# Sixteen products of a group's eight SSD heads in one block instead of two blocks of eight

## The chip, the cores and the metric

One core of a Trainium2 chip runs the kernel in one launch. The metric is the device time of that launch in microseconds. Beside it stands a profile: one execution taken by the hardware profiler. The engines are TensorE (PE, with its weight loads as PEld), VectorE (DVE), ScalarE (ACT), GpSimd (POOL) and SyncE (SP, which issues the DMAs of the weights).

## What is computed

The kernel computes a decoder layer for 256 tokens of width 1024, all in float32: a SwiGLU, then two branches side by side (a Mamba-2 SSD and differential attention) that are merged through gates, then a second SwiGLU, with norms around each. The change lies in the SSD. It has 32 heads of 64 channels in 4 groups of 8 heads, a state of 128, and two chunks of 128 tokens. The part of the reference that matters, cut to it:

```python
X = (x.astype(jnp.float32) * dt[..., None]).reshape(b, nc, Q, G, E, P)
...
Lmat = jnp.exp(jnp.where(causal, seg, -jnp.inf))
CB = jnp.einsum('bclgn,bcsgn->bgcls', Cc, Bc)
y_diag = jnp.einsum('bgcls,bgecls,bcsgep->bclgep', CB, Lmat, X)
...
return (y_diag + y_off).reshape(b, L, H, P)
...
y = (y + d_skip.astype(jnp.float32)[:, None] * xh.astype(jnp.float32)).astype(z.dtype)
```

With only two chunks the kernel does not carry a state from one to the other. It treats a head as causal attention over 256 tokens without a softmax: a head's matrix E (decay times CB, three 128 x 128 blocks, since the fourth is zero) is multiplied with the head's X, and the skip term is added.

## The kernel before

The weights come in chunks of 1 MB. Each chunk is split into a high part (`whi`, a cast on ACT, line 168) and a low part (`wlo`, a subtraction on DVE, line 171), so that float32 products are made of three faster ones. The projections run one chunk after another on PE: the convolved inputs `pxs`, then `pz` for the gate z in eight chunks (`pz00` to `pz31`, 48 matmuls each, lines 204 to 207), then `pq` and `pk` by turns, then the gates, and so on.

The SSD is background work beside these projections. `ssd_work` is a generator that is advanced between the chunks by a planner with a time budget: each `yield` tells how many microseconds of work the step is taken to be. For each of the 4 groups it does the following.

- It transposes the group's x on PE into `px` and multiplies with dt on DVE into `X` (lines 881, 882).
- For each half of the group, four heads, it loads a row of cumulated decays, broadcast over all partitions, into `acb` (a DMA issued by POOL, line 890).
- For each pair of heads it makes `E`: six small operations on ACT and DVE, one exponential over both heads on ACT (line 261), and one multiplication with the masked CB on DVE (line 904). The pool of E has 4 buffers (`K3_BUFS`).
- At the end of each half it multiplies: 8 products into one PSUM tile `py` (line 913; each product shows as two records in the profile), and adds the skip term on DVE with two operations per half (line 921).

While this stage is built, PE's order is left to the scheduler of the framework, which places each instruction by its own estimates. ACT's and DVE's orders come from it as well. The products of one half are tied together by order dependencies with the reason "together", so that the scheduler cannot put projection matmuls between them. The tile `py` comes from the PSUM pool `bg`, which has 5 buffers of one bank each; the same pool holds `px` and the scores of the attention. After the groups come `ssd_norm`, which multiplies with silu(z) and normalizes, and the attention.

Of the kernel before, what the change touches and what calls it, by code (L numbers as in the profile page):

```python
# [17 lines left out]
ALU = mybir.AluOpType  # L18
# [6 lines left out]
P = 128  # L25
T = 256
# [22 lines left out]
def tile_hybrid_layer(ctx: ExitStack, tc: tile.TileContext, x, ffn1_pre_g, ffn1_w_gate, ffn1_w_up,  # L49
# [4 lines left out]
    nc = tc.nc  # L54
# [5 lines left out]
    def k4(shape, name, dt=F32):  # L60
        return sb.tile(shape, dt, tag="k4", name=name, bufs=K4_BUFS)

    def k3(shape, name, dt=F32):
        return sb.tile(shape, dt, tag="k3", name=name, bufs=K3_BUFS)
# [18 lines left out]
    def bg(shape, name):  # L83
        return ps.tile(shape, F32, tag="bg", name=name, bufs=5)
# [166 lines left out]
    order = mybir.DependencyInfo(mybir.DependencyClass.NoSync, mybir.DependencyReason.DATA)  # L251
# [8 lines left out]
    def act(*args, **kw):  # L260
        a = nc.scalar.activation(*args, **kw)
        if act_fence[0] is not None:
            tc.add_manual_dep(a.ins, act_fence[0], order, reason="activation table")
        act_since.append(a.ins.name)
# [453 lines left out]
    cols_b = const.tile([P, 112], F32, name="cols_b")  # L718
# [51 lines left out]
    for jj in range(2):  # L770
        for a in (uh, ul):
            for i in range(4):
                k = i * 2 + jj
                nc.tensor.matmul(pdt[i * H_SSD:(i + 1) * H_SSD, :], wdt[:, k, :], a(k).bitcast(F32),
                                 start=jj == 0 and a is uh, stop=jj == 1 and a is ul)
# [94 lines left out]
    xs = [None] * 4  # L870
# [4 lines left out]
    def ssd_work(groups):  # L875
        for g in groups:
            X = k4([P, 2, 512], f"X{g}")
            for b in range(2):
                px = bg([P, 4, P], f"px{g}{b}")
                for c in range(4):  # L880
                    nc.tensor.transpose(px[:, c, :], xs[g][:, c, b * P:(b + 1) * P], ident)
                nc.vector.tensor_tensor(
                    X[:, b, :].rearrange("p (e q) -> p e q", q=64),
                    px.rearrange("p c (e q) -> p (c e) q", q=64),
                    dt[:, b, g * 8:(g + 1) * 8].unsqueeze(2).to_broadcast([P, 8, 64]), ALU.mult)
                yield 0.6
            for hf in range(2):
                acb = k4([P, 4, T], f"acb{g}{hf}")
                r0 = g * 8 + hf * 4
                nc.gpsimd.dma_start(acb, acd[r0:r0 + 4, :].partition_broadcast(P))  # L890
                py = bg([P, 2, T], f"py{g}{hf}")
                Es = []
                for pr in range(2):
                    E = k3([P, 2, 3 * P], f"E{g}{hf}{pr}")
                    for i in range(2):
                        hd = r0 + pr * 2 + i
                        lh = pr * 2 + i
                        act(E[:, i, :P], acb[:, lh, P:], AF.Relu, bias=acs[:, 1, hd:hd + 1])
                        nc.vector.tensor_scalar(E[:, i, P:T], acb[:, lh, :P], acs[:, 0, hd:hd + 1], 0.0,
                                                ALU.add, ALU.max)  # L900
                        act(E[:, i, T:], acb[:, lh, P:], AF.Exp, bias=acs[:, 2, hd:hd + 1], scale=-1.0)
                    act(E[:, :, :T], E[:, :, :T], AF.Exp, scale=-1.0)
                    Es.append(E)
                    nc.vector.tensor_tensor(E, E, cbm[g].unsqueeze(1).to_broadcast([P, 2, 3 * P]), ALU.mult)
                    yield 1.4

                last = None
                for pr in (1, 0):
                    for keys in range(2):
                        for i in range(2):  # L910
                            xc = slice((hf * 4 + pr * 2 + i) * 64, (hf * 4 + pr * 2 + i + 1) * 64)
                            o = py[i * 64:(i + 1) * 64, pr, keys * P:]
                            m = nc.tensor.matmul(o, X[:, keys, xc], Es[pr][:, i, (1 - keys) * P:(3 - 2 * keys) * P],
                                                 start=keys == 0, stop=keys == 1)
                            if last is not None:
                                tc.add_manual_dep(m.ins, last.ins.name, order, reason="together")
                            last = m
                for pr in range(2):
                    c = hf * 2 + pr
                    dc = 96 + g * 4 + c  # L920
                    nc.vector.scalar_tensor_tensor(xs[g][:, c, :], xs[g][:, c, :], cols_b[:, dc:dc + 1],
                                                   py[:, pr, :], ALU.mult, ALU.add)
                yield 0.8

    def ssd_norm(groups):

# [211 lines left out]
    for g in range(4):  # L1138
        xs[g] = k4([P, 4, T], f"xs{g}")
        for i in range(2):  # L1140
# [3 lines left out]
            back.run(0.4)  # L1144
    act_table(EXP_LN)
    back.add(ssd_work(range(4)))
    for g in range(4):
        sz[g] = k4([P, 4, T], f"sz{g}")
# [10 lines left out]
    for c in range(4):  # L1159
# [3 lines left out]
        o = (c % 2) * 2  # L1163
# [138 lines left out]
```

## Time and profile before

| | us |
|---|---|
| time, median of 3 runs | 745.24 (745.14 to 746.96) |
| the profiled execution | 745.16 |
| its span | 743.4 |
| PE busy | 734.7 |
| DVE busy | 524.9 |
| ACT busy | 441.3 |
| products of line 913, PE busy | 12.2 |

The profiled execution's own time is 1.76 us longer than its span; the sum of a forecast is made against that execution. In a row of the timeline the first number is the start in the span, the second the time from the first start to the last end of what is merged in the row; then come engine, line, operation, the tiles written and read, the shape and the count. Matmuls overlap in the pipeline: one may be shown as 0.28 us long while the next starts 0.12 us after it, so starts tell more than lengths. What stands in brackets at the end is the engine's idle time and what ended it. PE's weight loads have rows of their own.

### The profile page before, as it was taken

Reading aid. Unit: us, or ns where it says so; the run is one execution under the profiler, and the core shown is the slowest. Engines: PE = TensorE matmul, PEld = TensorE weight load, DVE = VectorE, ACT = ScalarE, POOL = GpSimd, SP = SyncE. Lnnn points to the kernel's source line nnn. Section 1 sums busy time; section 2 is a strip of 40 time slices with the busy share of each in tenths; the row PEclk is TensorE's granted clock in tenths of the full one; section 3 lists DMA queues with packets and bytes.
Section 4 is the critical chain, followed back from the end, with each engine's and each line's share of the span. In section 5 each row is a group of like instructions: output and inputs, shape, how many; then the busy total and the mean of one; then the engine's idle time right before and its main releaser. Section 6 shows DMA issues by size and latency. Waiting matters only on the chain.

```text
span 743.4 us, 11055 instructions
## 1 busy us (share of the span) xinstructions
PE 734.7 (99%) x4369; PEld 641.3 (86%) x4369; DVE 524.9 (71%) x807; ACT 441.3 (59%) x742; POOL 37.8 (5%) x72
## 2 busy tenths in 40 slices
PE   8999999999999999999999999999999999999996
PEld 6888888888889999999999888888888888888885
DVE  7986567654577888767888998684774867766612
ACT  6665557543566565957967666782664655665512
POOL 2700000000200000000000000000010000000000
PEclk9999999999999999999999999999999999999998
DMA  8884676486253647574656555364470767644701
GB/s 297 225 265 152 206 227 254 174 281 226 64 170 116 202 140 233 168 221 148 197 174 218 173 175 210 127 236 189 135 241 22 226 227 227 190 172 183 277 1 56
DMA packets 94212, 137.96 MB, mean 186 GB/s; under 512 B 2684, under 2 KB 68304, under 8 KB 94160
## 3 DMA queue, kind: packets, MB, share of 16 engines
q1 hardware_dynamic: 91488, 129.51, 52.9%
q0 software_dynamic: 2368, 7.22, 3.2%
q8 instruction: 34, 0.56, 0.3%
q10 hardware_dynamic: 304, 0.53, 0.2%
q14 instruction: 18, 0.15, 0.1%
HBM read 136.17 MB, written 1.08 MB: 185 GB/s over the span
## 4 chain that ended last, share of the span: by engine, by line
PE 98%; DMA 0%; DVE 0%; issue 0%; ACT 0%; DVEq 0%
PE acc_f L470 16%; PE pup_f L219 9%; PE pg_f L219 9%; PE pws L234 6%; PE pgt L234 6%; PE pg_f L218 4%; PE pup_f L218 4%; PE pn_f L244 3%; PE pn_f L234 3%; PE acc_mx L470 3%; PE pn_mx L234 3%; PE pwd L234 3%; PE pz L207 2%; PE pxs L207 2%; PE pz L205 2%; PE pz L204 2%
## 5 line engine op out<-in xcount | busy, mean ns | idle before, releaser
L171 DVE TENSOR_TENSOR wlo<-raw,whi 128x1024 fp32r<-128x1024 f32 (+1 forms) x246 | 290.9, 1211 | 55.7 <-ACT whi L168 54.6
L168 ACT CAST whi<-raw 128x1024 fp32r<-128x1024 f32 (+1 forms) x245 | 247.2, 1047 | 55.3 <-PE acc_f L470 21.7
L219 PE MATMUL pg_f<-u_f,whi 128*128 128x512 f32 x288 | 101.3, 396 | 0.0
L219 PE MATMUL pup_f<-u_f,whi 128*128 128x512 f32 x288 | 101.1, 396 | 0.0
L218 PE MATMUL pg_f<-u_f,wlo 128*128 128x256 f32 x252 | 70.6, 280 | 0.0
L218 PE MATMUL pup_f<-u_f,wlo 128*128 128x256 f32 x252 | 70.3, 279 | 0.0
L219 PEld LDWEIGHTS pg_f<-u_f,whi 128*128 128x128 f32 x288 | 52.8, 188 | 9.7
L219 PEld LDWEIGHTS pup_f<-u_f,whi 128*128 128x128 f32 x288 | 52.7, 188 | 9.8
L470 PE MATMUL acc_f<-whi,gh_f 128*128 128x512 f32 x176 | 58.1, 390 | 0.0
L470 PE MATMUL acc_f<-whi,gl_f 128*128 128x512 f32 x176 | 58.1, 389 | 0.0
L470 PE MATMUL acc_f<-wlo,gh_f 128*128 128x512 f32 x176 | 58.1, 389 | 0.0
L218 PEld LDWEIGHTS pg_f<-u_f,wlo 128*128 128x128 f32 x252 | 47.5, 189 | 1.7
L218 PEld LDWEIGHTS pup_f<-u_f,wlo 128*128 128x128 f32 x252 | 47.5, 189 | 1.6
L223 DVE TENSOR_TENSOR su_f<-pup_f,su_f 128x256 f32<-128x256 f32 x36 | 15.2, 421 | 40.5 <-ACT su_f L222 40.5
L470 PEld LDWEIGHTS acc_f<-wlo,gh_f 128*128 128x128 f32 x176 | 33.0, 188 | 6.9
L470 PEld LDWEIGHTS acc_f<-whi,gl_f 128*128 128x128 f32 x176 | 33.0, 188 | 6.8
L470 PEld LDWEIGHTS acc_f<-whi,gh_f 128*128 128x128 f32 x176 | 33.0, 188 | 6.7
L234 PE MATMUL pgt<-whi,u_mx 128*128 128x512 f32 x128 | 33.1, 393 | 0.0
L222 ACT COPY su_f<-pup_f 128x256 f32<-128x256 f32 x36 | 13.4, 371 | 31.4 <-PE pup_f L219 31.2
L204 PE MATMUL pxs<-u_mx,whi 128*128 128x256 f32 x128 | 31.7, 285 | 0.0
L204 PE MATMUL pz<-u_mx,whi 128*128 128x256 f32 x128 | 31.6, 284 | 0.0
L205 PE MATMUL pz<-u_mx,whi 128*128 128x256 f32 x128 | 31.4, 283 | 0.0
(310 smaller groups left out, 1433.6 us busy)
## 6 DMA issues: line engine op xcount, KB each, us to landing
raw<-in_w_in_dram SPq DMA_DIRECT2D x40, 1024.0 KB, 5.4
raw<-in_ffn_w_down_dram SPq DMA_DIRECT2D x22, 1024.0 KB, 5.1
raw<-in_ffn_w_gate_dram SPq DMA_DIRECT2D x20, 1024.0 KB, 6.0
raw<-in_ffn_w_up_dram SPq DMA_DIRECT2D x20, 1024.0 KB, 5.4
raw<-in_ssd_w_branch_dram SPq DMA_DIRECT2D x8, 1024.0 KB, 5.1
acb<-acd POOLq DMA_DIRECT2D x8, 512.0 KB, 4.9
raw<-in_da_w_branch_dram SPq DMA_DIRECT2D x4, 1024.0 KB, 5.1
raw<-in_w_out_dram SPq DMA_DIRECT2D x4, 1024.0 KB, 4.9
```

The lines of the kernel that those rows point to most:

```text
L168: copy(hi[:, js, :], r[:, q * nj + j:q * nj + j + n, :])
L171: nc.vector.tensor_sub(lo[:, js, :], r[:, q * nj + j:q * nj + j + n, :], hi[:, js, :].bitcast(F32))
L204: nc.tensor.matmul(acc[m], wh(j)[:, cs], ah(k0 + j), start=first and j == ks[0], stop=False)
L205: nc.tensor.matmul(acc[m], wh(j)[:, cs], al(k0 + j), start=False, stop=False)
L207: nc.tensor.matmul(acc[m], wl(j)[:, cs], ah(k0 + j), start=False, stop=last and j == ks[-1])
L218: nc.tensor.matmul(acc[:, :T], wl(j)[:, cs], ah(j), start=False, stop=False)
L219: nc.tensor.matmul(acc, wh(j)[:, cs], ahl(j), start=j == 0, stop=j == KD - 1)
L222: nc.scalar.copy(dst[:, m, :], acc[:, T:])
L223: nc.vector.tensor_tensor(dst[:, m, :], acc[:, :T], dst[:, m, :], ALU.add)
L234: nc.tensor.matmul(acc, a(k0 + j), b(j), start=first and i == 0, stop=last and i == 11)
L244: nc.tensor.matmul(accs[b], x_(k0 + j), w_(j), start=first and j == 0 and w_ is wh and x_ is acts[b][0], stop=last and j == 3 and w_ is wl)
L470: nc.tensor.matmul(acc[b][q], x_[:, ts], w_(kt)[:, halves[q]], start=i == 0 and kt == 0 and x_ is ah and w_ is wh, stop=i == n - 1 and kt ...
```

## The change

The list of E is now kept for the whole group, so all four E (eight heads) are made first. Then two `py` tiles are taken and the group's 16 products are issued in one chain of order dependencies, from the last pair of heads to the first. The four additions of the skip term follow in the same order. The number of products, their operands and sizes are the same; the planner's two steps of 0.8 become one of 1.6.

```diff
+            Es = []
             for hf in range(2):
                 acb = k4([P, 4, T], f"acb{g}{hf}")
                 r0 = g * 8 + hf * 4
                 nc.gpsimd.dma_start(acb, acd[r0:r0 + 4, :].partition_broadcast(P))
-                py = bg([P, 2, T], f"py{g}{hf}")
-                Es = []
                 for pr in range(2):
...
-                last = None
-                for pr in (1, 0):
-                    for keys in range(2):
-                        for i in range(2):
-                            xc = slice((hf * 4 + pr * 2 + i) * 64, (hf * 4 + pr * 2 + i + 1) * 64)
-                            o = py[i * 64:(i + 1) * 64, pr, keys * P:]
-                            m = nc.tensor.matmul(o, X[:, keys, xc], Es[pr][:, i, (1 - keys) * P:(3 - 2 * keys) * P],
-                                                 start=keys == 0, stop=keys == 1)
-                            if last is not None:
-                                tc.add_manual_dep(m.ins, last.ins.name, order, reason="together")
-                            last = m
-                for pr in range(2):
-                    c = hf * 2 + pr
-                    dc = 96 + g * 4 + c
-                    nc.vector.scalar_tensor_tensor(xs[g][:, c, :], xs[g][:, c, :], cols_b[:, dc:dc + 1],
-                                                   py[:, pr, :], ALU.mult, ALU.add)
-                yield 0.8
+            py = [bg([P, 2, T], f"py{g}{hf}") for hf in range(2)]
+            last = None
+            for c in (3, 2, 1, 0):
+                for keys in range(2):
+                    for i in range(2):
+                        xc = slice((c * 2 + i) * 64, (c * 2 + i + 1) * 64)
+                        o = py[c // 2][i * 64:(i + 1) * 64, c % 2, keys * P:]
+                        m = nc.tensor.matmul(o, X[:, keys, xc], Es[c][:, i, (1 - keys) * P:(3 - 2 * keys) * P],
+                                             start=keys == 0, stop=keys == 1)
+                        if last is not None:
+                            tc.add_manual_dep(m.ins, last.ins.name, order, reason="together")
+                        last = m
+            for c in (3, 2, 1, 0):
+                dc = 96 + g * 4 + c
+                nc.vector.scalar_tensor_tensor(xs[g][:, c, :], xs[g][:, c, :], cols_b[:, dc:dc + 1],
+                                               py[c // 2][:, c % 2, :], ALU.mult, ALU.add)
+            yield 1.6
```

## The prediction

> **What bounds the kernel.** First the page's busy shares and its chain of work that ended last; then all instructions that touch the tile `py`, then the timeline of TensorE around one block of products, for prices.
>
> ```profile
> span 743.4 us, 11055 instructions
> PE 734.7 (99%) x4369; PEld 641.3 (86%) x4369; DVE 524.9 (71%) x807; ACT 441.3 (59%) x742; POOL 37.8 (5%) x72
> PE   8999999999999999999999999999999999999996
> PE 98%; DMA 0%; DVE 0%; issue 0%; ACT 0%; DVEq 0%
> ```
>
> TensorE (PE) is the bound: it is busy for 99% of the span and carries 98% of the chain. Time changes only where PE's own steps change, or where PE begins to wait. In the stretch of the edit it does not wait at all but once:
>
> ```profile
> 291.70:401.00 109.30, 109.19 (x934) 104.53 (x934) 85.32 (x134) 81.86 (x149) 4.24 (x8) 1.00 0.60 186
> L913 PE MATMUL py<-E,X x128: 272/326/430, 306.7 to 374.7; 128*64 128x256 f32 x64, 128*64 128x128 f32 x64
> 304.13 0.28 PE L204 MATMUL pz<-u_mx,whi 128*128 128x256 f32 x1
> 306.05 0.52 PE L207 MATMUL pz<-u_mx,wlo 128*128 128x256 f32 x3
> 306.68 1.52 PE L913 MATMUL py<-E,X 128*64 128x256 f32 x16
> 324.74 0.52 PE L207 MATMUL pz<-u_mx,wlo 128*128 128x256 f32 x3
> 325.18 1.52 PE L913 MATMUL py<-E,X 128*64 128x256 f32 x16
> 326.63 0.86 PE L207 MATMUL pz<-u_mx,wlo 128*128 128x256 f32 x5
> 327.33 0.28 PE L204 MATMUL pz<-u_mx,whi 128*128 128x256 f32 x1
> ```
>
> The first row is one stretch of 109.30 us (columns: bounds, length, busy PE, weight loads, DVE, ACT, POOL, clock, DMA share, GB/s): PE 109.19 busy at full clock. The 64 products are 128 records, two each, in 8 blocks of 16. Three ordinary matmuls take 0.52 from first start to last end and one takes 0.28, so the step from start to start is (0.52 - 0.28) / 2 = 0.12. Before the block at 325.18 the last ordinary matmul starts at 324.74 + 0.24 = 324.98 and the block follows 0.20 later; at 306.68 it follows 306.29 by 0.39. The 0.19 too much is the one wait, for the mask product of E.
>
> **The change, part by part.** Nothing is computed that was not computed before. In the changed program's order on PE, eight blocks of 8 products have become four of 16, with nothing between: group 0's after 11 matmuls of `pz11`, group 1's after 39 of `pz21`, group 2's after 30 of `pq0`, group 3's after 44 of `pk1`.
>
> Price of entering and leaving a block. From 324.74 to 327.33 PE does 8 ordinary matmuls (0.96) and one block: 2.59 - 0.96 = 1.63. The steady cost inside, from narrow windows of the same block:
>
> ```profile
> 325.67 0.60 PE L913 MATMUL py<-E,X 128*64 128x128 f32 x5
> 325.78 0.49 PE L913 MATMUL py<-E,X 128*64 128x128 f32 x4
> 325.88 0.39 PE L913 MATMUL py<-E,X 128*64 128x256 f32 x2
> 326.43 0.27 PE L913 MATMUL py<-E,X 128*64 128x128 f32 x1
> ```
>
> Each row's start counts here. Narrow products step by 0.11 (325.67, 325.78), also into the first wide one of the second pair of heads at 325.88. That pair runs from 325.88 to its last product at 326.43, plus one step of 0.11: 0.66, or 0.65 with the rounding of the starts. Two pairs cost 1.31, so 0.32 of the 1.63 is the switch in and out. By pieces: entry 0.20 for 0.12; first pair 0.70 (325.18 to 325.88) for 0.65; exit 0.20 (326.43 to 326.63) for 0.11; the five matmuls behind take (0.86 - 0.28) / 4 = 0.145 a step for 0.12, 0.10 in all. That adds to 0.32 or 0.33; I take 0.33. A merged block pays it once where two paid it twice: 4 x 0.33 = 1.32 less. The inner seam (c = 2 to c = 1) has no row; its ends are 0 (like the seam between pairs at 325.88) and 0.33 (as if left and entered again). I take 0, since both sides are products of the same shape; only the output bank differs.
>
> The Trainium skill's page "TensorEngine Tiling (Array Packing)", section "Key Properties", says that changing the tiling mode, not just the tile, drains TensorE; ordinary matmuls use all 128 columns, these 64. "TensorE: Matmul & The Clock Gate", section "Single matmul latency", gives a lone warm matmul a constant of 166 ns above its streaming; two exposed per block would be an estimate of 0.33, and eight fewer 1.33. By a rule without a drain the sum would be 0; the row of 1.63 against 1.31 agrees with the drain.
>
> Transposes. Before, two of the four `px` blocks stand right behind a `py` block; after, one.
>
> ```profile
> 297.51 1.04 PE L881 MATMUL px<-ident,xs 128*128 128x128 f32 x8
> 298.30 0.36 PE L204 MATMUL pz<-u_mx,whi 128*128 128x256 f32 x1
> 311.80 1.52 PE L913 MATMUL py<-E,X 128*64 128x256 f32 x16
> 313.25 1.09 PE L881 MATMUL px<-ident,xs 128*128 128x128 f32 x8
> 314.10 0.36 PE L204 MATMUL pz<-u_mx,whi 128*128 128x256 f32 x1
> 314.30 0.28 PE L205 MATMUL pz<-u_mx,whi 128*128 128x256 f32 x1
> ```
>
> Together they take 314.10 - 311.80 = 2.30; apart 326.63 - 325.18 = 1.45, 298.30 - 297.51 = 0.79 and the 0.10 behind the block, 2.34 (the 0.20 to the second matmul, 0.08 too much, is paid either way). One adjacency lost costs 0.04. Sum on PE: 1.32 - 0.04 = 1.28 less, if PE arrives at no block before its E is ready.
>
> **Is E ready?** The first product of a merged block uses the last E of the group, so one wait covers four E. What ACT and DVE need:
>
> ```profile
> 303.75 1.27 ACT L261 ACTIVATE E<-acb,acs 128x128 f32<-128x128 f32 x4
> 304.92 0.62 ACT L261 ACTIVATE E<-E 128x512 f32<-128x512 f32 x1
> 305.44 0.57 ACT L1152 COPY sz<-pz 128x512 f32<-128x512 f32 x1
> 305.90 1.06 ACT L168 CAST whi<-raw 128x1024 fp32r<-128x1024 f32 x1
> 306.86 1.28 ACT L261 ACTIVATE E<-acb,acs 128x128 f32<-128x128 f32 x4
> 320.14 0.59 ACT L1152 COPY sz<-pz 128x512 f32<-128x512 f32 x1 [3.85 <-PE pz L207]
> 305.57 0.96 DVE L904 TENSOR_TENSOR E<-E,cbm 128x768 f32<-128x768 f32 x1 [0.34 <-ACT E L261]
> 310.38 0.96 DVE L904 TENSOR_TENSOR E<-E,cbm 128x768 f32<-128x768 f32 x1 [0.28 <-ACT E L261]
> ```
>
> By starts, one E takes ACT 1.17 + 0.52 = 1.69, a copy 0.47, a split 0.96. DVE's mask product (0.96) starts 0.03 after the exponential. At 306.68 PE starts 0.15 after the mask's end at 306.53.
>
> - Group 0: without the block at 306.68, `pz10` ends at 304.13 + 48 x 0.12 = 309.89; 11 more matmuls and the entry give 311.30. The last mask product still ends at 310.38 + 0.96 = 311.34, as ACT's order before it is the same; PE starts at 311.49. Wait 0.19: the one of 306.68, moved.
> - Group 1: the block takes 0.05 + 4 x 0.65 + 0.10 to the first transpose (314.24), the transposes 0.85 (315.09), 37 matmuls 4.44 + 0.08: `pz20` begins at 319.61, 0.33 before now. 48 + 39 matmuls and the entry: PE arrives at 330.14. ACT starts from the copy at the end of `pz11`, now at 320.14, then 319.81: copy, split, three E, copy, one E take 0.47 + 0.96 + 5.07 + 0.47 + 1.79 (the last exponential to its end) = 8.76, so 328.57; the mask ends at 329.56. Spare 0.58.
> - Group 2: the block 2.75 (332.89), 9 matmuls 1.18, transposes 0.79, `pz30` 5.84 (340.70), `pz31` 5.76 (346.46), 30 matmuls and entry: PE at 350.15. ACT's last copy of z can begin when `pz31` has ended, at about 346.66 (0.20 after its last step, as 319.81 is to 319.61); before that it has done what stands ahead (from 340.90 a copy, an exponential, three splits and one E: 0.47 + 0.52 + 2.88 + 1.69 = 5.56). Copy 0.47, one E 1.79, mask 0.99: 349.91. Spare 0.24.
> - Group 3: block 2.75, 18 matmuls 2.26, transposes 0.79, 48 + 48 + 44 matmuls with 0.08 and entry: PE at 372.92. ACT is through with group 2 at 348.9; then
>
> ```profile
> 351.30 1.28 ACT L254 ACT_TABLE_LOAD   x1
> 352.59 3.90 ACT L261 ACTIVATE sz<-sz 128x1024 f32<-128x1024 f32 x4
> 356.51 1.28 ACT L254 ACT_TABLE_LOAD   x1
> ```
>
> 6.5 for these (355.4), five splits and a square of about a split's length, a copy each of q and k, and four E: 6 x 0.96 + 2 x 0.47 + 4 x 1.69 + 0.1 = 13.6, so 369.0; masks for two E on DVE, 371 at the latest. Spare over 1.
>
> Other queues. Four E buffers now stay taken until the whole group's block is done (c = 0 last): group 1's first E is written from 321.2, its block 0 ends at 314.3; groups 2 and 3 have over 3 us. POOL's broadcasts of `acb` are tied to other releases:
>
> ```profile
> L890 POOL DMA_DIRECT2D acb<-acd x8: 527/530/569, 285.5 to 355.6; - x8
> DMA to landing us min/median/max: 3.8/4.9/6.9
> L921 DVE SCALAR_TENSOR_TENSOR xs<-xs,cols_b,py x16: 472/478/483, 308.4 to 375.4; 128x256 f32<-128x256 f32 x16
> ```
>
> Group 2's second one now waits for block 1's last product (332.7): landed by 339.6 at the slowest, used from 344.8. SP's weight loads follow DVE's splits; group 1's E stand ahead of the splits of chunk 56, by about 3 us, and chunk 56 is first used at 340.7, some 8 us after its split. The four evictions of a group (4 x 0.48) come together instead of two and two; behind them on DVE stand the mask of X and splits with microseconds to spare. I cost all this at nothing; with that cover gone, an E late by x costs PE x.
>
> **Sum.** The profiled execution took 745.16 (743.4 span, 1.76 around it): 745.16 - 1.28 = 743.88, call it 743.9. The median of the runs, 745.24, stands 0.08 above it.
>
> **Rivals.**
> 1. The seam is paid like an exit and entry: the 0.33 comes back in each block, and the time is 745.16 + 0.04 = 745.2. For it: the output bank changes there. Against: in the block at 325.18 nothing happens at the seam between its pairs, which also changes E and X.
> 2. The other side, slower: the last E comes late. Place: group 2, spare 0.24 (group 1: 0.58). If ACT or DVE puts one more E's work (1.79 + 0.99 = 2.78) between, PE waits 2.54 there: 743.88 + 2.54 = 746.4; in group 1 too, 748.6. It decides once the waits sum to more than 1.28. Against: the order on both engines is known and the prices scatter by hundredths.
> 3. More is freed than the switches. PE is idle for 743.4 - 734.7 = 8.7 us; were 1.5 of it tied to this stage coming late, the time would be 742.4. Against: the slices show PE at 9 in all but the first and the last, so the idle time lies at the ends.
> 4. That the products do not stand together is excluded by the order.
>
> **Chances and range.** As forecast, 743.6 to 744.3: 0.74. Rival 1: 0.09. Rival 2: 0.07 (0.06 of it beyond 747.4). Rival 3: 0.10. The range 743.4 to 745.6 holds the first two. A difference of 0.3% (2.2 us) is about what a measurement of this kernel can tell from none; forecast and rival 1 lie within it. Faster 0.10, same 0.84, slower 0.06.
>
> **What would show it.** Right: four blocks of 32 records, each about 2.82 long from first start to last end (1.52 + 1.30), PE waiting about 0.2 at the first alone, and `pq2` starting some 1.3 us earlier. Wrong: a step of 0.2 or more in the middle of a block, a wait of PE on the mask product of groups 1 to 3, or PE busy time down by much more than 1.3.

## The result and the profile after

| | before | after |
|---|---|---|
| time, median of 20 runs each, us | 745.23 (744.95 to 746.96) | 743.92 (743.48 to 746.10) |
| the profiled execution, us | 745.16 | 743.95 |
| its span, us | 743.4 | 742.2 |

After over before is 0.9983, with a 95% interval from 0.9976 to 0.9990: 1.3 us less, a difference that the runs resolve although it lies under the 0.3% that the prediction took for the limit. The forecast was 743.9.

The page of the changed kernel: its busy shares, the chain of work that ended last, and then the stretch from the first `pz` on, with the columns of the stretch shown before.

```profile
span 742.2 us, 11061 instructions
PE 734.1 (99%) x4369; PEld 641.7 (86%) x4369; DVE 525.2 (71%) x807; ACT 441.1 (59%) x742; POOL 38.0 (5%) x72
...
PE 98%; DMA 1%; issue 0%; DVE 0%; SPq 0%; DVEq 0%; ACT 0%
...
291.90:400.00 108.10, 108.08 (x935) 104.45 (x934) 86.08 (x134) 82.18 (x149) 4.23 (x8) 1.00 0.61 189
```

PE is the bound as before, at full clock in the stretch. Its instructions are as many as before (4369); what became less is the time that they take. Where the gain arises is seen from the start of the first `pz` to the start of the first `acc_mx`, a matmul behind the whole stage. From the rows of these two tiles, before (first fence) and after (second); the first start stands behind the three durations:

```profile
L204 PE MATMUL pz<-u_mx,whi x128: 278/283/364, 291.7 to 345.9; 128*128 128x256 f32 x128
L470 PE MATMUL acc_mx<-whi,mh x32: 389/389/477, 528.9 to 551.9; 128*128 128x512 f32 x32
```

```profile
L204 PE MATMUL pz<-u_mx,whi x128: 278/283/362, 291.9 to 345.3; 128*128 128x256 f32 x128
L470 PE MATMUL acc_mx<-whi,mh x32: 389/389/477, 527.7 to 550.6; 128*128 128x512 f32 x32
```

528.9 - 291.7 = 237.2 before, 527.7 - 291.9 = 235.8 after: 1.4 less. Below, this stretch is called "the stage". The first `pz` itself starts 0.2 later in the profile of after, so the span shows 1.2. PE's busy time in the stage, before and after (bounds, length, busy time, count, then clock, DMA share and GB/s):

```profile
291.75:528.94 237.19, 237.08 (x1578) 1.00 0.56 182
291.94:527.71 235.77, 235.75 (x1578) 1.00 0.56 183
```

It fell by 1.33 there, so a switch counts as busy time of PE; PE's idle time in the stage fell from 0.11 to 0.02.

The four blocks, from the timeline of PE (start in the span, time to the last end, engine, line, operation, tiles, shape, count):

```profile
311.28 0.28 PE L204 MATMUL pz<-u_mx,whi 128*128 128x256 f32 x1
311.58 2.82 PE L913 MATMUL py<-E,X 128*64 128x256 f32 x32
...
315.38 0.28 PE L204 MATMUL pz<-u_mx,whi 128*128 128x256 f32 x1
...
330.01 0.28 PE L204 MATMUL pz<-u_mx,whi 128*128 128x256 f32 x1
330.22 2.82 PE L913 MATMUL py<-E,X 128*64 128x256 f32 x32
...
333.19 1.12 PE L207 MATMUL pz<-u_mx,wlo 128*128 128x256 f32 x8
334.15 1.04 PE L881 MATMUL px<-ident,xs 128*128 128x128 f32 x8
334.94 0.36 PE L204 MATMUL pz<-u_mx,whi 128*128 128x256 f32 x1
...
350.22 2.82 PE L913 MATMUL py<-E,X 128*64 128x256 f32 x32
...
372.98 2.82 PE L913 MATMUL py<-E,X 128*64 128x256 f32 x32
...
376.31 0.28 PE L204 MATMUL pq<-u_mx,whi 128*128 128x256 f32 x1
```

From 330.01 to 334.15 PE does ten ordinary matmuls (1.20) and one block: 4.14 - 1.20 = 2.94. Two blocks of 8 cost 2 x 1.63 = 3.26 before, or 3.28 where one is taken as 1.64, as the starts give it before rounding. So a merged group saves 0.32 to 0.34, and four 1.3 to 1.4. Inside the block, around the seam between the two `py` tiles (narrow windows of the same timeline, where each row's start counts):

```profile
331.46 1.58 PE L913 MATMUL py<-E,X 128*64 128x128 f32 x18
331.57 1.47 PE L913 MATMUL py<-E,X 128*64 128x256 f32 x16
```

With 16 of 32 records left, at 331.57, the second tile begins, 0.11 behind the start before it, the step that the narrow products have elsewhere in a block. The seam costs nothing.

When E was ready (DVE's mask product of the last E of groups 0 to 3):

```profile
310.57 0.96 DVE L903 TENSOR_TENSOR E<-E,cbm 128x768 f32<-128x768 f32 x1 [0.73 <-ACT E L261]
328.72 0.96 DVE L903 TENSOR_TENSOR E<-E,cbm 128x768 f32<-128x768 f32 x1 [1.22 <-ACT E L261]
349.05 0.96 DVE L903 TENSOR_TENSOR E<-E,cbm 128x768 f32<-128x768 f32 x1 [0.84 <-ACT E L261]
370.87 0.96 DVE L903 TENSOR_TENSOR E<-E,cbm 128x768 f32<-128x768 f32 x1 [0.22 <-ACT E L261]
```

The ends are 311.53, 329.68, 350.01 and 371.83, and PE starts its blocks at 311.58, 330.22, 350.22 and 372.98. In group 0 PE starts 0.30 behind the last ordinary matmul where 0.21 is the entry without a wait (330.01 to 330.22): a wait of 0.09. In the others PE starts 0.54, 0.21 and 1.15 behind the end of the mask product.

### The profile page after: what moved, and what is told of

Its sections match the earlier page's. It is cut to its first block, busy times and chain, and to the rows that moved or that the text cites. A ratio compares the mean times of both kernels' runs of the same rounds, so it can differ in the third digit from the quotient of the medians.

```text
span 742.2 us, 11061 instructions
## 1 busy us (share of the span) xinstructions
PE 734.1 (99%) x4369; PEld 641.7 (86%) x4369; DVE 525.2 (71%) x807; ACT 441.1 (59%) x742; POOL 38.0 (5%) x72
## 3 DMA queue, kind: packets, MB, share of 16 engines
HBM read 136.17 MB, written 1.08 MB: 185 GB/s over the span
## 4 chain that ended last, share of the span: by engine, by line
PE 98%; DMA 1%; issue 0%; DVE 0%; SPq 0%; DVEq 0%; ACT 0%
PE acc_f L470 16%; PE pup_f L219 9%; PE pg_f L219 9%; PE pws L234 6%; PE pgt L234 6%; PE pg_f L218 4%; PE pup_f L218 4%; PE pn_f L244 3%; PE pn_f L234 3%; PE acc_mx L470 3%; PE pn_mx L234 3%; PE pwd L234 3%; PE pz L205 2%; PE pxs L207 2%; PE pz L207 2%; PE pxs L205 2%
```

## The experiments

Ten kernels were run, each timed beside the kernel before on the same chip. That kernel's median was 745.26 beside the cut, its control and the two kernels of full width, 745.15 beside the blocks of four products, the block of two groups, its control and the kernel without the pause, and 745.22 beside the last two; so a difference between medians of two of these sets is uncertain by about 0.1. Two theories are set against each other. By the first, the gain is four fewer switches of PE in and out of the products, at 0.33 each. By the second, something else became less when the E of eight heads are collected first.

### One ordinary matmul in the middle of each block

Everything stays as in the changed kernel, but each block is cut once.

```diff
+                if c == 1:
+                    m = nc.tensor.matmul(py[0][:, 1, :P], ones_r, ones_r, start=True, stop=True)
+                    tc.add_manual_dep(m.ins, last.ins.name, order, reason="together")
+                    last = m
```

> The changed kernel with one ordinary 128-column float32r matmul put into the middle of each group's chain of 16 products; its result is overwritten by the next product, so the layer is computed as before. Switch theory (every change between ordinary matmuls and the 64-column products costs PE 0.33 us in and out): each block is cut in two, so the four blocks give back 4 x (0.33 + 0.06 for the matmul itself) = 1.6 us: about 745.5, with steps of 0.2 in the middle of each block. Rival (the gain came from the new places of the blocks, or from fewer waits on E): only 4 x 0.06 = 0.2 us more than the changed kernel, 744.1.

Measured: 745.29, ratio to before 1.0003 (0.9994 to 1.0012). From PE's timeline of this kernel, group 1:

```profile
330.77 0.28 PE L204 MATMUL pz<-u_mx,whi 128*128 128x256 f32 x1
330.98 1.52 PE L917 MATMUL py<-E,X 128*64 128x256 f32 x16
332.43 0.33 PE L910 MATMUL py<-ones_r 128*128 128x128 f32 x1
...
334.36 0.88 PE L207 MATMUL pz<-u_mx,wlo 128*128 128x256 f32 x6
```

From the last ordinary matmul ahead to the second behind it is 334.36 - 330.77 = 3.59, where the whole block has 333.19 - 330.01 = 3.18. One matmul of 128 columns and 128 rows to stream costs 0.41 there, and with four of them the time is back at that of the kernel before.

### The control: two more products of the same shape there

```diff
+                if c == 1:
+                    for i in range(2):
+                        m = nc.tensor.matmul(py[0][i * 64:(i + 1) * 64, 1, P:], X[:, 1, c * 128 + i * 64:c * 128 + (i + 1) * 64],
+                                             Es[c][:, i, :P], start=True, stop=True)
```

> The control of the cut: instead of the ordinary matmul, two extra 64-column products of the block's own kind (both overwritten by the next products, nothing else changed). Both theories: one more step of 0.11 us in each of the four blocks, 0.44 us over the changed kernel, 744.4. If any extra instruction in the chain cost a third of a microsecond, it would be 745.2 or more.

Measured: 744.76, ratio 0.9994 (0.9985 to 1.0003), 0.84 above the changed kernel. PE's timeline, group 1:

```profile
330.50 0.28 PE L204 MATMUL pz<-u_mx,whi 128*128 128x256 f32 x1
...
332.06 0.39 PE L911 MATMUL py<-E,X 128*64 128x128 f32 x4
...
333.90 1.12 PE L207 MATMUL pz<-u_mx,wlo 128*128 128x256 f32 x8
```

333.90 - 330.50 = 3.40, 0.22 above the whole block. The expected 744.4 missed by 0.36, since I had priced the two products, four records, at one step of 0.11; four times 0.22 is 0.88, near the 0.84 of the medians. So four records of the block's own kind cost 0.22 and one ordinary matmul costs 0.41: the block pays for a change to another kind of matmul, not for an instruction more. The foreign matmul differs in width and in data type; the full-width kernels below tell these apart.

### Blocks of four products

The kernel before with 16 blocks: each pair of heads multiplies on its own.

```diff
-                last = None
-                for pr in (1, 0):
+                    last = None
...
-                            m = nc.tensor.matmul(o, X[:, keys, xc], Es[pr][:, i, (1 - keys) * P:(3 - 2 * keys) * P],
+                            m = nc.tensor.matmul(o, X[:, keys, xc], E[:, i, (1 - keys) * P:(3 - 2 * keys) * P],
...
-                yield 0.8
+                    yield 0.4
```

> The kernel before with each pair's four products right behind its own E: sixteen blocks of 4 products instead of eight of 8, everything computed. Switch theory: eight more switches at 0.33 us, 745.2 + 2.7 = 747.9, and the blocks' own work unchanged. Rival (gain from places and waits): PE waits for E differently, but no cost per block: 745.2, or more only by waits on the mask product that the trace then shows.

Measured: 747.82, ratio 1.0037 (1.0025 to 1.0050), 2.67 slower than before. In its timeline:

```profile
307.89 0.28 PE L205 MATMUL pz<-u_mx,whi 128*128 128x256 f32 x1
308.10 0.87 PE L909 MATMUL py<-E,X 128*64 128x256 f32 x8
308.90 1.22 PE L207 MATMUL pz<-u_mx,wlo 128*128 128x256 f32 x8
309.96 0.28 PE L204 MATMUL pz<-u_mx,whi 128*128 128x256 f32 x1
```

307.89 to 309.96 holds nine ordinary matmuls (1.08) and one block: 0.99, of which one pair's own cost is 0.65 and 0.34 the switch. The medians say the same: (747.82 - 745.15) / 8 = 0.33 for each block from 8 to 16, and (745.23 - 743.92) / 4 = 0.33 from 4 to 8.

### Products of full width

In two kernels one product of 128 columns stands where a pair of heads has two of 64. These kernels leave out the products of each pair's second head. One has eight blocks as before, the other four as after, whose edit is shown. The data type, and its change at the block's ends, stays the same.

```diff
-                    for i in range(2):
-                        xc = slice((c * 2 + i) * 64, (c * 2 + i + 1) * 64)
-                        o = py[c // 2][i * 64:(i + 1) * 64, c % 2, keys * P:]
+                    for i in range(1):
+                        xc = slice(c * 128, (c + 1) * 128)
+                        o = py[c // 2][:, c % 2, keys * P:]
```

> The kernel before with 128-column products: of each pair of heads only the first head's E is used, with the X of both heads, so the second head's products are left out and half of the SSD output is not the layer's. E is still made for all heads. Two 64-column products run side by side in the time of one, so the work per block should last the same 1.30 us. If the switch cost comes from the column tiling, it is gone: 8 x 0.33 = 2.6 us less than the kernel before, 742.5. If it comes from changing between float32r and float32 matmuls, it stays: 745.2.

> The changed kernel with the same 128-column products (second heads' products left out). Column tiling as the cause: the same 742.5 as with eight blocks, since there is nothing left to save by merging. Change of type as the cause: 743.9, 1.3 less than with eight blocks.

Measured: 743.38 with eight blocks (0.9976, 0.9966 to 0.9985) and 742.89 with four (0.9969, 0.9957 to 0.9981). From PE's timeline, first with four blocks (group 0, then group 1), then with eight:

```profile
311.09 0.28 PE L204 MATMUL pz<-u_mx,whi 128*128 128x256 f32 x1
311.38 2.88 PE L913 MATMUL py<-E,X 128*128 128x256 f32 x16
...
329.73 0.28 PE L204 MATMUL pz<-u_mx,whi 128*128 128x256 f32 x1
329.85 2.78 PE L913 MATMUL py<-E,X 128*128 128x256 f32 x16
...
332.58 1.12 PE L207 MATMUL pz<-u_mx,wlo 128*128 128x256 f32 x8
```

```profile
324.22 0.52 PE L207 MATMUL pz<-u_mx,wlo 128*128 128x256 f32 x3
324.65 1.58 PE L913 MATMUL py<-E,X 128*128 128x256 f32 x8
...
334.82 1.47 PE L913 MATMUL py<-E,X 128*128 128x256 f32 x8
336.13 1.04 PE L881 MATMUL px<-ident,xs 128*128 128x128 f32 x8
```

At full width the block starts one ordinary step behind the matmul ahead (329.73 to 329.85: 0.12), and 332.58 - 329.73 = 2.85 stands against 3.18 for the same stretch of the changed kernel: 0.33 less. So the switch is that of the column width. These kernels also issue half as many products, but that is not what saves the 0.33: blocks of half that length show the same difference (1.31 from 334.82 to 336.13, where a block of the kernel before costs 1.63). The change of data type alone, which is still there, costs nothing at the entry.

Both times are above the expected 742.5, and they differ by 0.49 where the theory had them equal. With four blocks, group 0's starts 0.29 behind the matmul ahead, not 0.12; with eight, the block at 324.65 starts 0.19 behind 324.46. This is PE at the block before its E is there, now that it comes earlier. The mask product of the block at 324.65 shows it:

```profile
323.63 0.96 DVE L904 TENSOR_TENSOR E<-E,cbm 128x768 f32<-128x768 f32 x1 [0.73 <-ACT E L261]
```

It ends at 324.59, and PE follows 0.06 later. By the starts in the trace, such a block is also longer inside: the second record comes 0.32 behind the first, where the step is 0.22 in a block that finds its E ready (the one at 368.66). Of eight blocks four wait for E, of four only group 0's. With eight blocks the stage took 235.3 (527.0 - 291.7), 1.9 less than before where 2.6 was expected; the waits, 0.3 more than before, and the longer first steps, 0.4, account for the missing 0.7.

### Eight heads more in a block, and its control

Two groups share a block: two blocks of 32 products. E then needs 8 buffers (`K3_BUFS`), for which `K4_BUFS` goes from 29 to 26; the control is the changed kernel with that smaller pool alone.

```diff
-        for g in groups:
+        for g0 in groups[::2]:
+            for g in (g0, g0 + 1):
...
+            todo = [(g, c) for g in (g0 + 1, g0) for c in (3, 2, 1, 0)]
+            for g, c in todo:
```

> The 32 products of two groups in one block, two blocks in all, with 8 buffers of E for 4 and 26 buffers of the large pool for 29 to make room. Switch theory: two switches fewer than the changed kernel, 2 x 0.33 = 0.7 us, less 0.05 for one adjacency with the transposes: 743.3. Rival (late E): the first E of the third group waits for nothing new, but the last E of a pair of groups comes later; if PE waits there for one E's work, 743.3 + 2.8 = 746.1. Fewer large buffers could hold up the splits; the next run prices that alone.

> The changed kernel with 26 large buffers for 29 and nothing else: the price of the room that two groups in a block need. PE's order is the same. If the splits stay ahead of PE by several us as now, 743.9; if a split comes late, more, with a wait of PE on a low or high part of a weight.

Measured: 742.92, ratio 0.9974 (0.9963 to 0.9986); the control 743.94, ratio 0.9981 (0.9972 to 0.9990), that is the changed kernel's own time. The block of two groups:

```profile
323.85 0.28 PE L204 MATMUL pz<-u_mx,whi 128*128 128x256 f32 x1
324.06 5.42 PE L915 MATMUL py<-E,X 128*64 128x256 f32 x64
...
329.63 1.12 PE L207 MATMUL pz<-u_mx,wlo 128*128 128x256 f32 x8
```

329.63 - 323.85 = 5.78 stands for two times 3.18 less the two ordinary steps that are counted twice: 6.36 - 0.24 = 6.12, so 0.34 less. Two such savings are 0.68, and this block does not wait for E (0.21 at the entry). The stage took 235.1 here (526.7 - 291.6), 0.7 less than in the changed kernel. The median is 1.0 below the control's and 0.4 below the expected 743.3; what of this lies outside the stage is not explained. This is the fastest kernel that computes everything, 2.2 below the kernel before.

### Transposes behind every block

The price of 0.04 for an adjacency of transposes and products was to be tested by taking out the pause that the planner gets behind a block, in all groups.

```diff
-            yield 1.6
```

> The changed kernel without the planner's step behind a group's products, so that the next group's transposes stand right behind the block in all three cases (after: one of three). By the price of an adjacency, 2 x 0.05 = 0.1 us less than the changed kernel: 743.8. The whole background runs some 1.6 us of the planner's time earlier per group, so a wait on E could come instead; each would show as a start of a block more than 0.21 behind the matmul before it.

Measured: 747.08, ratio 1.0029 (1.0018 to 1.0039). The expectation was wrong, and by more than the change had gained. The transposes of groups 1 to 3 do stand behind a block; the loss is elsewhere. PE's waits of this kernel (what waited, for what; total, times, longest), and then the chain of work in that place:

```profile
PE pq L204 <- ACT whi L168: 1.8, 1, 1.8
```

```profile
...
357.66 1.28 ACT L254
...
358.95 3.90 ACT sz L261 x4
...
362.86 1.28 ACT L254
...
364.15 1.05 ACT whi L168
...
```

The scheduler, given the background steps earlier, put group 3's E and the silu of z with its two table loads on ACT ahead of a split, the second half of the chunk that `pq1` is made of. The chain runs from ACT's split, ended at 365.20, straight to PE. The stage grew by 2.6; this wait is 1.8 of it. Of the other 0.8, a wait of PE's weight loads for DVE makes up 0.5: it stands in the last scores of the attention (`psc`, at 466.38), and the changed kernel's trace has no such wait. The rest stays open.

To test this, the pause was taken out in part, so that the split stays ahead of the silu in one kernel and another split falls behind it in the other.

```diff
-            yield 1.6
+            if g >= 2:
+                yield 1.6
```

> The changed kernel without the planner's pause of 1.6 behind the block of groups 0 and 1 alone, so that the transposes of group 2 stand right behind a block as those of group 1 do, while the second half of chunk 59's high part stays ahead of group 3's E and of the silu of z on ACT. If the loss of the run without any pause came from that late split, PE has no wait on a split here, and the time is 743.85 (one adjacency more, 0.05 less). If the loss came from the adjacency itself or from the steps being earlier, one of two removed pauses' worth comes back: about 745.4.

```diff
-            yield 1.6
+            if g != 2:
+                yield 1.6
```

> The changed kernel without the pause of 1.6 behind the block of group 2 alone. Group 3's transposes stand right behind a block. On ACT the second half of chunk 60's high part now stands behind one E, the silu of z with its two table loads (6.5) and two more E. By the prices of the trace ACT comes to it at 356.2 + 0.5 + 0.96 + 1.69 + 6.5 + 2 x 1.69 = 369.2 and has it at 370.2, where PE wants it at about 368.5 (pk1 begins three chunks of 5.76 after 350.2). If a late split costs PE what it is late, PE waits 1.7 there and the time is 743.9 - 0.05 + 1.7 = 745.6. If the split of the other run was not the cause, the time is 743.85.

Measured: 743.57, ratio 0.9979 (0.9970 to 0.9989), and 746.04, ratio 1.0015 (1.0005 to 1.0026). The second one, ACT's timeline and then PE's:

```profile
361.05 3.90 ACT L261 ACTIVATE sz<-sz 128x1024 f32<-128x1024 f32 x4
...
369.65 1.03 ACT L168 CAST whi<-raw 128x1024 fp32r<-128x1024 f32 x1
```

```profile
368.66 0.28 PE L205 MATMUL pk<-u_mx,whi 128*128 128x256 f32 x1
370.73 0.39 PE L204 MATMUL pk<-u_mx,whi 128*128 128x256 f32 x1 [1.79 <-ACT whi L168]
```

ACT came to the split at 369.65 where 369.2 was worked out, and PE waited 1.79 where 1.7 was; the median came out 0.4 above the expected 745.6. With the split ahead of the silu there is no such wait, though two blocks more have transposes right behind them (group 2's eight, and four of group 3's eight). The loss is the late split. The adjacency itself is too small for the medians: the ratios 0.9979 and 0.9983 (of the changed kernel) lie within each other's intervals.

## Why the prediction was right

- **The bound.** PE has 98% of the chain after as before, and the time followed PE's steps: shown.
- **The switch, 0.33 a block.** 0.32 to 0.34 by the starts around the blocks, 0.33 by the medians of 16, 8 and 4 blocks, and given back by one foreign matmul in the middle. The rule of the Trainium skill's page "TensorEngine Tiling (Array Packing)", section "Key Properties", that a change of the tiling mode drains TensorE, agrees with the full-width kernels, where the 0.33 of a block goes away when the products use all columns. That the cost is a drain, and not another part of the switch, no run shows. The trace does show that the weights come later: at 330.22 the first weight load of the narrow block starts together with its first product, while in the full-width block at 372.11 it starts 0.12 ahead of it (371.99).
- **The seam, taken as 0.** 0.11 from start to start at 331.57. Rival 1 (745.2) is out.
- **The transposes, 0.04.** After, block and transposes together take 315.38 - 311.58 = 3.80 in group 0; apart, in group 1, 333.19 - 330.22 = 2.97 and 334.94 - 334.15 = 0.79 with the same 0.20 behind. That is 3.96 with one ordinary matmul more (0.12): 0.04. Right in size.
- **E.** Forecast: a wait of 0.19, then 0.58, 0.24 and over 1 to spare; found: a wait of 0.09, then 0.54, 0.21 and 1.15. The wait was half of what was worked out: the mask product ended as forecast (311.34, and 311.53 with the 0.19 by which this trace runs late), but PE followed 0.05 behind it, where the prediction had taken the 0.15 of 306.68. With the step ahead of the block at 0.30 for 0.39 before, that is worth 0.09. Rival 2 did not occur; what a late operation of ACT costs PE was seen (1.8 us of waiting) in the two kernels with a split behind the silu, but a late E of group 2 itself was not forced.
- **The other queues at nothing.** Nothing in the stage waits on PE's side but the 0.09.
- **Rival 3.** It is out: four switches and the wait of group 0 make up the whole of the stage's gain. PE's busy time in the stage fell by 1.33; in the whole span it fell by only 0.6 (734.7 to 734.1), because PE was busy 0.7 longer ahead of the stage (289.33 and 290.06), which the change doesn't touch.
- **The sum.** The blocks are 2.82 long each, as forecast. Stage: 4 x 0.34 = 1.36 less, 0.09 of waiting less, 0.04 more, 1.41 together, against 1.4 measured and 1.28 forecast. The profiled execution fell by 1.21, as the start of the program, which the change doesn't touch, took 0.2 longer in it; the medians fell by 1.31. The mechanism was right. That the profiled time came out within 0.1 of the forecast is partly luck: in the stage the switches gave 0.04 more than forecast and the wait 0.09 more, and the later start took 0.2 back.

`pq2` was to start 1.3 earlier and did by 1.2 in the span (377.54 in the trace of before, 376.31 here), 1.4 against the first `pz`.

## What to carry to other kernels

When TensorE is the bound, count how often its order goes between matmuls of full and of narrow column width, and price one such pair of switches from the starts around one block: here 0.33 us, and gathering paid off from sixteen blocks down to two. PE's busy time over the whole span is a poor measure of it, as it also holds what differs ahead of the stage. Before moving such work, work out when its last operand is ready and when PE comes to it. And look at what an earlier background step pushes behind it on the other engines: the split of half a weight chunk, put behind a silu, cost more than all the switches saved.

## What the runs showed of the hardware that was not expected

- Two products of 64 columns side by side cost what one of 128 columns costs. A block with 16 records of full width and one with 32 of half width differ by 0.33 (2.85 and 3.18 for the same stretch), and blocks of half that size by 0.32 (1.31 and 1.63): the difference doesn't grow with the products.
- A single small foreign matmul in a block costs 0.41. With 0.06 for the matmul itself, an estimate from half the ordinary step of 0.12, 0.35 is left for the switch there and back.
- PE began a block 0.05 to 0.15 after the end of the mask product that it waited for: 311.53 to 311.58 after, 306.53 to 306.68 before.
- Going from the projections' pieces (fp32r) to float32 products of the same width shows no cost of its own at the entry: 0.12, the ordinary step.
- The start of the program varies between profiled executions, in kernels that don't differ there: the first `pz` began at 291.7 before and 291.9 after, as the stage's rows show. A gain near 1 us is better read from a stretch of the trace, or from medians, than from one span.
